# Delta rule of block 2: in-chunk products as 64x64 on the diagonal quarters of TensorE

## The chip, the core and the metric

The kernel runs on one core of a Trainium2 chip. The metric is the device time of one execution in microseconds; the time before is the median of three runs.

## The reference, cut to what matters

Two layers of block 1 and then two layers of block 2 work on x of 512 tokens by 1024. Block 2 mixes three branches (a dilated attention, a convolution, and a gated delta rule with 4 heads of 128 channels) and then has a gated feed-forward. The change is in the delta rule, which works in chunks of 64 tokens:

```python
def chunk_gated_delta_rule(q, k, v, g, beta):
    ...
    C = GDN_CHUNK                       # 64
    ...
    decay = jnp.exp(jnp.where(lower_incl, g[..., :, None] - g[..., None, :], -jnp.inf))
    k_beta = k * beta[..., None]
    v_beta = v * beta[..., None]
    m = jnp.where(strict, jnp.einsum('bhncd,bhnsd->bhncs', k_beta, k) * decay, 0.0)
    rhs = jnp.concatenate([v_beta, k_beta * jnp.exp(g)[..., None]], axis=-1)
    sol = lax.linalg.triangular_solve(m + jnp.eye(C, dtype=jnp.float32), rhs, left_side=True, lower=True,
                                      unit_diagonal=True)
    u = sol[..., :Dv]
    w = sol[..., Dv:]
    intra = jnp.where(lower_incl, jnp.einsum('bhncd,bhnsd->bhncs', q, k) * decay, 0.0)

    def step(state, xs):
        q_c, k_c, u_c, w_c, g_c, intra_c = xs
        v_new = u_c - w_c @ state
        out = (q_c * jnp.exp(g_c)[..., None]) @ state + intra_c @ v_new
        ...
```

## The kernel before

All activations lie transposed, 128 channels on the partitions by 512 tokens. A dense product is three matmuls per 128x128 weight tile, high and low parts in fp32r (`mm3`, L307 to L309); the weights come in on SP's queue and are split by ScalarE (L285) and VectorE (L286). The delta rule and the attention work in plain fp32, where one matmul leaves two records in the trace; a transpose leaves one.

Block 2's mixing (`block2_mix`) is a set of generators that a `Driver` runs while the program is built. Dense jobs (26 projections of one layer, then the output projection) yield after every three matmuls, foreground generators after every step, with the TensorE time and the latency they are assumed to have (`yield 430, 600`). The driver takes the foreground step that is due with the smallest priority number, else a dense step. So it sets TensorE's order: the steps of the delta rule stand between pieces of dense products. PSUM gives 3 tiles to dense products and 5 to everything else (`pm`).

A `Half` is two heads. Its queries, keys and values go through a short convolution on VectorE (`gdn_conv`) and through transposes (L555). `intra(b)` then works on one block of 128 tokens (two chunks) and both heads, at most two such chains at a time, four chains a half: decays from the gates (L1090), the scores k k^T and k q^T as whole 128x128 products (L1103, L1111), of which a mask leaves the two diagonal 64x64 quarters, and five levels that double the size of the inverted triangular blocks. TT is the transposed inverse; in each level it is transposed (L1118, copied to T by ScalarE, L1120), W = m T is formed (L1124, copied, L1126), then W TT (L1130), and VectorE writes it into TT under a mask (L1131). At the end w (L1136) and u (L1141) are formed. GpSimd scales the decays (L1096, L1098) and makes the first TT from m (L1107, L1108).

`rec` takes the 8 chunks of a half in order: w times the state (L1165), subtracted from u, the state's update (L1173), q times the state (L1186, scaled by VectorE, L1189), and after two chunks the score product (L1195). `out` transposes a head's result back (L1218). `ab_post` prepares the gates at the start of the layer.

## Time and profile before

| | us |
|---|---|
| median of three runs | 2601.34 (2600.72 to 2603.84) |
| profiled execution, its time | 2604.12 |
| its span | 2602.3 |
| TensorE (PE) busy | 2523.3 |
| its weight loads (PEld) | 2061.3 |
| VectorE (DVE) busy | 1535.7 |
| ScalarE (ACT) busy | 1027.9 |
| GpSimd (POOL) busy | 518.0 |

The span is what the profiler saw from the first to the last instruction. A record's duration is from its start to its modelled end; the next matmul may start well before that end, so the distance between two starts tells what a matmul takes of TensorE's time. "128\*64" in a row is rows by columns of the array in use, the shape behind it the data that stream through. The two layers' mixing stages of block 2 lie at about 1140 to 1440 us and 1880 to 2170 us.

### The profile page before, as it was taken

To read this page: it belongs to the slowest core of one execution; us is meant where nothing else is said; L and a number is where in the kernel's file an instruction comes from. 1 tells how busy PE (TensorE), PEld (TensorE's weight loads), DVE (VectorE), ACT (ScalarE), POOL (GpSimd) and SP (SyncE) were. 2 spreads that over 40 slices of the span, in tenths; PEclk is the share of its full clock that TensorE was granted. 3 is DMA by queue.
4 is the path that set the end of the run, shared out by engine and by line. 5 is a ranking of instruction groups with operands and counts; after the bars stand their busy time and mean duration, and the time that the engine had idled before them with its cause. 6 is when DMAs were issued, how large, how long until landed. Compare 5 with 4: busy or idle time off the path is not lost. (4 is left out here: it accounts for less than half of the span.)

```text
span 2602.3 us, 33506 instructions
## 1 busy us (share of the span) xinstructions
PE 2523.3 (97%) x12988; PEld 2061.3 (79%) x12988; DVE 1535.7 (59%) x2380; ACT 1027.9 (39%) x1715; POOL 518.0 (20%) x465
## 2 busy tenths in 40 slices
PE   8999999999999999999999999999899999999998
PEld 6777888878778888877777888888777778888887
DVE  6777666336776665356898554432678885744323
ACT  4554333223644333234345432222443355522221
POOL 3332111003231111013220221100221311311101
PEclk9999999999999999999999999999999999999999
DMA  4113222332022223321111222223211112222232
GB/s 165 41 42 110 96 96 96 92 103 82 33 76 95 98 97 95 116 93 40 57 41 63 84 98 97 97 91 99 96 57 41 41 49 98 82 97 97 96 95 77
DMA packets 69854, 216.05 MB, mean 83 GB/s; under 512 B 8256, under 2 KB 11968, under 8 KB 69696
## 3 DMA queue, kind: packets, MB, share of 16 engines
q1 hardware_dynamic: 68336, 212.40, 24.4%
q8 instruction: 102, 1.67, 0.3%
q10 hardware_dynamic: 1360, 1.52, 0.2%
q14 instruction: 56, 0.46, 0.1%
HBM read 207.60 MB, written 6.29 MB: 82 GB/s over the span
## 5 line engine op out<-in xcount | busy, mean ns | idle before, releaser
L307 PE MATMUL pd<-hh,wh 128*128 128x512 f32 (+1 forms) x2064 | 800.5, 391 | 12.3 <-ACT wh L285 8.1
L308 PE MATMUL pd<-hl,wh 128*128 128x512 f32 (+1 forms) x2064 | 800.6, 389 | 7.0 <-DVE hl L525 4.4
L309 PE MATMUL pd<-hh,wl 128*128 128x512 f32 (+1 forms) x2064 | 796.0, 388 | 0.9 <-DVE wl L286 0.9
L285 ACT CAST wh<-wr 128x1024 fp32r<-128x1024 f32 (+2 forms) x407 | 400.7, 986 | 976.2 <-PE pd L308 927.4
L286 DVE TENSOR_TENSOR wl<-wr,wh 128x1024 fp32r<-128x1024 f32 (+2 forms) x407 | 471.4, 1160 | 398.7 <-ACT wh L285 389.1
L308 PEld LDWEIGHTS pd<-hl,wh 128*128 128x128 f32 x2064 | 389.7, 189 | 84.1 <-DVE hl L525 7.5
L307 PEld LDWEIGHTS pd<-hh,wh 128*128 128x128 f32 x2064 | 387.3, 189 | 87.1 <-ACT wh L285 8.1
L309 PEld LDWEIGHTS pd<-hh,wl 128*128 128x128 f32 x2064 | 388.9, 189 | 75.2 <-DVE wl L286 2.0
L309 PE MATMUL pd<-gh,wl 128*128 128x512 f32 (+1 forms) x704 | 269.0, 382 | 0.0
L308 PE MATMUL pd<-gl,wh 128*128 128x512 f32 (+1 forms) x704 | 269.0, 382 | 0.0
L307 PE MATMUL pd<-gh,wh 128*128 128x512 f32 (+1 forms) x704 | 268.8, 382 | 0.0
L309 PEld LDWEIGHTS pd<-gh,wl 128*128 128x128 f32 x704 | 132.6, 188 | 28.3
L308 PEld LDWEIGHTS pd<-gl,wh 128*128 128x128 f32 x704 | 132.6, 188 | 28.3
L307 PEld LDWEIGHTS pd<-gh,wh 128*128 128x128 f32 x704 | 132.6, 188 | 28.3
L1550 POOL TENSOR_TENSOR fz<-fz,nrB 128x512 f32<-128x512 f32 x44 | 77.6, 1764 | 365.6 <-ACT fz L1549 365.6
L864 POOL TENSOR_TENSOR fy<-fy,fy 128x512 f32<-128x512 f32 x44 | 56.7, 1288 | 383.2 <-DVE fy L858 367.5
L1557 DVE TENSOR_TENSOR fz<-pd,fz 128x512 f32<-128x512 f32 x42 | 29.0, 691 | 138.4 <-PE pd L309 135.4
L854 DVE TENSOR_TENSOR fh<-pd,nrB 128x512 f32<-128x512 f32 x88 | 60.5, 687 | 59.8 <-PE pd L309 54.9
L533 POOL TENSOR_TENSOR nacc<-nacc,nsq 128x512 f32<-128x512 f32 x30 | 46.2, 1540 | 240.7 <-ACT nsq L532 240.1
L1368 DVE SCALAR_TENSOR_TENSOR cz<-cy,dwh,cz 128x501 f32<-128x501 f32 (+21 forms) x120 | 89.1, 752 | 1.2 <-ACT cz L1366 0.3
L1548 DVE TENSOR_TENSOR fz<-pd,nrB 128x512 f32<-128x512 f32 x42 | 28.8, 690 | 102.7 <-PE pd L309 102.7
L856 ACT ACTIVATE fy<-fh,cols 128x512 f32<-128x512 f32 x88 | 71.9, 817 | 35.9 <-DVE fh L854 35.9
(400 smaller groups left out, 3530.1 us busy)
## 6 DMA issues: line engine op xcount, KB each, us to landing
wr<-in_w_up_dram SPq DMA_DIRECT2D x132, 512.0 KB, 3.2
wr<-in_w_in_dram SPq DMA_DIRECT2D x80, 512.0 KB, 3.3
wr<-in_w_down_dram SPq DMA_DIRECT2D x64, 512.0 KB, 3.5
wr<-in_w_gate_dram SPq DMA_DIRECT2D x44, 512.0 KB, 3.2
wr<-in_w_down_dram SPq DMA_DIRECT2D x32, 384.0 KB, 3.1
wr<-in_w_o_dram SPq DMA_DIRECT2D x32, 256.0 KB, 2.8
wr<-in_w_out_dram SPq DMA_DIRECT2D x16, 512.0 KB, 3.3
xd<-x SPq DMA_DIRECT2D x16, 256.0 KB, 2.0
```

Source lines behind the costliest of these rows:

```text
L285: nc.scalar.copy(out=hi[:, cs], in_=raw[:, cs])
L286: nc.vector.tensor_tensor(lo[:, cs], raw[:, cs], hi[:, cs].bitcast(F32), ALU.subtract)
L307: nc.tensor.matmul(ps, wh, xhi, start=start, stop=False)
L308: nc.tensor.matmul(ps, wh, xlo, start=False, stop=False)
L309: nc.tensor.matmul(ps, wl, xhi, start=False, stop=stop)
L533: (nc.vector if last else nc.gpsimd).tensor_tensor(self.acc, self.acc, sq, ALU.add)
L854: nc.vector.tensor_tensor(h, ps, F.rB, ALU.mult)
L856: nc.scalar.activation(out=y, in_=h, func=AF.Identity, scale=col("cw1", tt), bias=col("cb", tt))
L864: nc.gpsimd.tensor_tensor(y, y, part.pop(t), ALU.mult)
L1368: nc.vector.scalar_tensor_tensor(zt[:, s:], y[:, :S - s], w(30 - s), zt[:, s:], ALU.mult, ALU.add)
L1550: nc.gpsimd.tensor_tensor(z, z, F.rB, ALU.mult)
L1557: nc.vector.tensor_tensor(z, ps, z, ALU.mult)
```

## The change

- `intra` works on two blocks (four chunks) and both heads in one chain, so a half has two chains instead of four. Of every product only the diagonal quarters are formed: eight 64x64 matmuls for two blocks, two chunks and two heads, with row r of the array's halves in turn. A tile of 256 columns holds the four blocks of one product.
- T and TT stand side by side in one tile (`both`). T comes once from TT by a product with the identity; after that each level forms W TT and TT W (16 matmuls, one masked copy of 512 columns), so that T needs no transpose in the next level.
- The decays of a half are made at once for all blocks (`decays`): one 128x512 product, and VectorE, GpSimd and ScalarE instructions of 512 columns.
- A head with odd number has its two chunks of each block swapped (`swap`): its convolution's result is written in two half-width instructions. So in one step of `rec` the two heads lie on different halves of the partitions and stand on different halves of the array.
- In `rec` both heads' shares of a chunk are 128 columns wide, on 128 partitions together; the update of the state goes into two PSUM tiles, and the scaling of q times the state goes from VectorE to ScalarE. `out` takes both heads of a half.

The diff, cut to its core:

```diff
...
+        ab, sw = tl(K, "z", 3), tl(K, "z", 3)
...
+        for c in range(2):
+            nc.scalar.copy(out=swap(sw[:64, :], c), in_=swap(ab[:64, :], 1 - c))
...
-    def gdn_conv(ps, j, tag, bufs):
+    def gdn_conv(ps, j, tag, bufs, odd):
...
-        tanh_silu2(K, th, y)
+        if not odd:
+            tanh_silu2(K, th, y)
+            return th
+        for c in range(2):
+            nc.scalar.activation(out=swap(th, c), in_=swap(y, 1 - c), func=AF.Tanh, scale=0.5)
+        for c in range(2):
+            nc.vector.scalar_tensor_tensor(swap(th, c), swap(th, c), 1.0, swap(y, 1 - c), ALU.add, ALU.mult)
...
-        def intra(self, b):
+        def decays(self):
...
+            of = lambda q: sl[self.hp][:, 8 * q:8 * q + 8].rearrange("p (n o) -> p n o", o=1).to_broadcast([128, 8, 64])
+            yield lambda: st.ab and (self.hp == 0 or halves[0].begun[1])
+            steps = tl(K, "sq", 1)
+            nc.gpsimd.tensor_tensor(e64(steps), of(0), row(K.tri64), ALU.mult)
+            yield 0, 2000
+            ps = ps_m(K)
+            nc.tensor.matmul(ps, K.same, steps, start=True, stop=True)
+            dd = tl(K, "dd", 1, n=1024)
+            dn, dt_ = dd[:, :512], dd[:, 512:]
+            nc.vector.tensor_tensor(e64(dt_), e64(ps), of(1), ALU.subtract)
+            nc.gpsimd.tensor_tensor(e64(dt_), e64(dt_), row(K.mk), ALU.add)
+            nc.scalar.activation(out=dt_, in_=dt_, func=AF.Exp)
+            nc.gpsimd.tensor_tensor(e64(dt_), e64(dt_), of(2), ALU.mult)
+            nc.gpsimd.tensor_tensor(e64(dn), e64(dt_), row(K.nstrict), ALU.mult)
+            self.dd = dd.rearrange("p (a n) -> p a n", a=2)
+            yield 860, 7000
...
+        def intra(self, bp):
             hp = self.hp
...
+            at = [(bl, c, r) for bl in range(2) for c in range(2) for r in range(2)]
+            rows = lambda r: slice(64 * r, 64 * r + 64)
+            cell = lambda bl, c: slice((2 * bl + c) * 64, (2 * bl + c) * 64 + 64)
...
+            toks = lambda bl, r: slice((2 * bp + bl) * 128 + 64 * r, (2 * bp + bl) * 128 + 64 * r + 64)
...
+            yield lambda: (st.intra < 2 and self.dd is not None and self.nk == 2 and self.q[1] is not None and
+                           (bp == 0 or self.begun[0]))
             st.intra += 1
...
             knT, q = self.knT, self.q
+            both = tl(K, "TT", 2)
+            TT, T = both[:, :256], both[:, 256:]
+            nc.gpsimd.tensor_tensor(r44(TT), K.id64.rearrange("p (o j) -> p o j", o=1).to_broadcast([128, 4, 64]),
+                                    K.id64.rearrange("p (o j) -> p o j", o=1).to_broadcast([128, 4, 64]), ALU.mult)
             pk = ps_m(K)
...
+            for n, other in enumerate((knT, q)):
+                for bl, c, r in at:
+                    h = r ^ c
+                    nc.tensor.matmul(pk[rows(r), 256 * n:256 * n + 256][:, cell(bl, c)], knT[h][:, toks(bl, r)],
+                                     other[h][:, toks(bl, r)], start=True, stop=True)
+            ma = tl(K, "AT", 3)
+            nc.vector.tensor_tensor(ma.rearrange("p (a n) -> p a n", a=2), pk.rearrange("p (a n) -> p a n", a=2),
+                                    self.dd[:, :, bp * 256:bp * 256 + 256], ALU.mult)
+            mT, self.AT[bp] = ma[:, :256], ma[:, 256:]
+            nc.vector.copy_predicated(r44(TT), K.pairs, r44(mT))
+            yield 900, 2000
+            p0 = ps_m(K)
+            for bl, c, r in at:
+                nc.tensor.matmul(p0[rows(r), cell(bl, c)], TT[rows(r), cell(bl, c)],
+                                 K.ident[rows(r), rows(r)], start=True, stop=True)
+            nc.scalar.copy(out=T, in_=p0[:, :256])
+            yield 430, 600
             for lv in range(5):
-                p0 = ps_m(K)
-                for h in range(2):
-                    nc.tensor.transpose(p0[:, hs[h]], TT[:, hs[h]], K.ident)
-                T = bt("T", 2)
-                nc.scalar.copy(out=T, in_=p0[:, :256])
-                yield 218, 600
                 pw = ps_m(K)
-                for h in range(2):
-                    nc.tensor.matmul(pw[:, hs[h]], mT[:, hs[h]], T[:, hs[h]], start=True, stop=True)
-                W = bt("W", 2)
+                for bl, c, r in at:
+                    nc.tensor.matmul(pw[rows(r), cell(bl, c)], mT[rows(r), cell(bl, c)], T[rows(r), cell(bl, c)],
+                                     start=True, stop=True)
+                W = tl(K, "W", 2, n=256)
                 nc.scalar.copy(out=W, in_=pw[:, :256])
                 yield 430, 600
                 pb = ps_m(K)
-                for h in range(2):
-                    nc.tensor.matmul(pb[:, hs[h]], W[:, hs[h]], TT[:, hs[h]], start=True, stop=True)
-                nc.vector.copy_predicated(r2(TT), K.lvl(lv), r2(pb[:, :256]))
-                yield 430, 700
+                for n, (x, y) in enumerate(((W, TT), (TT, W)) if lv < 4 else ((W, TT),)):
+                    for bl, c, r in at:
+                        nc.tensor.matmul(pb[rows(r), 256 * n:256 * n + 256][:, cell(bl, c)], x[rows(r), cell(bl, c)],
+                                         y[rows(r), cell(bl, c)], start=True, stop=True)
+                w = 512 if lv < 4 else 256
+                four = lambda t: t[:, :w].rearrange("p (a n j) -> p a n j", n=4, j=64)
+                nc.vector.copy_predicated(four(both), K.lvl(lv), four(pb))
+                yield 860 if lv < 4 else 430, 1000
             yield lambda: self.nv == 2
+            for bl, c, r in at:
+                nc.tensor.matmul(pu[rows(r), wide(bl, c)], TT[rows(r), cell(bl, c)],
+                                 self.v[r ^ c][rows(r), blk(bl)], start=True, stop=True)
+            self.U[bp] = tl(K, "u", 2)
+            nc.scalar.copy(out=self.U[bp], in_=pu)
+            pw = [ps_m(K), ps_m(K)]
+            for bl, c, r in at:
+                nc.tensor.matmul(pw[r][:, cell(bl, c)], self.kg[r ^ c][rows(r), blk(bl)],
+                                 TT[rows(r), cell(bl, c)], start=True, stop=True)
+            self.WT[bp] = tl(K, "wT", 2)
+            for r in range(2):
+                nc.scalar.copy(out=self.WT[bp][:, 256 * r:256 * r + 256], in_=pw[r][:, :256])
...
                 for c in range(2):
...
+                    rows = [slice(64 * (h ^ c), 64 * (h ^ c) + 64) for h in range(2)]
+                    order = (c, 1 - c)
+                    vf = self.U[bp][:, (2 * bl + c) * 128:(2 * bl + c) * 128 + 128]
+                    cell = slice((2 * bl + c) * 64, (2 * bl + c) * 64 + 64)
                     if s is not None:
                         pv = ps_m(K)
...
+                        for h in order:
+                            r = h ^ c
+                            nc.tensor.matmul(pv[rows[h], :128], self.WT[bp][:, 256 * r:256 * r + 256][:, cell],
                                              s[:, hs[h]], start=True, stop=True)
...
+                        nc.vector.tensor_tensor(vf, vf, pv[:, :128], ALU.subtract)
+                        yield 220, 500
                     if not (b == NB - 1 and c == 1):
...
+                        pst = [ps_m(K), ps_m(K)]
+                        for h in order:
+                            nc.tensor.matmul(pst[h][:, :128], self.kd[h][rows[h], bs], vf[rows[h], :],
                                              start=True, stop=True)
                         ns = bt("st", 2)
...
+                        for h in range(2):
+                            if s is None:
+                                nc.vector.tensor_copy(out=ns[:, hs[h]], in_=pst[h][:, :128])
+                                continue
+                            j = 16 * (h ^ c) + 4 * b + 2 * hp + h
+                            nc.vector.scalar_tensor_tensor(ns[:, hs[h]], s[:, hs[h]], egl[:, j:j + 1],
+                                                           pst[h][:, :128], ALU.mult, ALU.add)
                     if s is not None:
                         p1 = ps_m(K)
...
+                        for h in order:
+                            nc.tensor.matmul(p1[rows[h], :128], self.q[h][:, bs][:, rows[h]], s[:, hs[h]],
+                                             start=True, stop=True)
+                        nc.scalar.activation(out=o[:, hs[c]], in_=p1[:, :128], func=AF.Copy,
+                                             scale=sl[hp][:, 24 + 2 * b + c:25 + 2 * b + c])
                     s = ns
...
+                    yield 440, 300
                 p2 = ps_m(K)
...
+                for c in range(2):
+                    for r in (slice(0, 64), slice(64, 128)):
+                        cell = slice((2 * bl + c) * 64, (2 * bl + c) * 64 + 64)
+                        nc.tensor.matmul(p2[r, hs[c]], self.AT[bp][r, cell],
+                                         self.U[bp][r, (2 * bl + c) * 128:(2 * bl + c) * 128 + 128],
+                                         start=True, stop=True)
...
     for hf in halves:
-        for b in range(NB):
-            drv.spawn(hf.intra(b), 1)
+        drv.spawn(hf.decays(), 1)
+        for bp in range(2):
+            drv.spawn(hf.intra(bp), 1)
         drv.spawn(hf.rec(), 0)
...
```

The order of TensorE's instructions in the first half's chains, layer 1 of block 2, two chains in turn. Names are output, then data and weights; 128x512 rows are the dense products. Before, it reads:

```order
L1124 MATMUL pm_9658<-T_9649,mT_9591 128x128 x2
L1118 MATMUL pm_9663<-cst,TT_9606 128x128 x2
L307 MATMUL pd_9629<-hh_8808,wh_9530 128x512
L308 MATMUL pd_9629<-hl_8809,wh_9530 128x512
L1130 MATMUL pm_9671<-TT_9593,W_9661 128x128 x2
L1124 MATMUL pm_9675<-T_9666,mT_9604 128x128 x2
L309 MATMUL pd_9629<-hh_8808,wl_9531 128x512
L307 MATMUL pd_9629<-hh_8901,wh_9530 128x512
L1118 MATMUL pm_9683<-cst,TT_9593 128x128 x2
L1130 MATMUL pm_9688<-TT_9606,W_9678 128x128 x2
```

Before, transposes, W and W TT of the two chains are single pairs of 128x128 between dense pieces. After the change TensorE has in the same place:

```order
L309 MATMUL pd_9848<-hh_9087,wl_9562 128x512
L1167 MATMUL pm_9801<-TT_9579,AT_9598 64x64 x8
L1175 MATMUL pm_9812<-TT_9601,W_9784 64x64 x8
L1175 MATMUL pm_9812<-W_9784,TT_9601 64x64 x8
L1175 MATMUL pm_9830<-TT_9579,W_9810 64x64 x8
L1175 MATMUL pm_9830<-W_9810,TT_9579 64x64 x8
L1167 MATMUL pm_9852<-TT_9601,AT_9620 64x64 x8
L307 MATMUL pd_9848<-hh_9180,wh_9561 128x512
L308 MATMUL pd_9848<-hl_9181,wh_9561 128x512
L1167 MATMUL pm_9863<-TT_9579,AT_9598 64x64 x8
L309 MATMUL pd_9848<-hh_9180,wl_9562 128x512
```

Instead of L1118, L1124 and L1130 there are groups of eight 64x64 for W (L1167) and for the two products of a level (L1175, two rows each), and the transposes are gone.

The recurrence on TensorE, one chunk of the first half. Before, it reads:

```order
L1165 MATMUL pm_9999<-st_9985,wT_9876 64x128
L1118 MATMUL pm_10003<-cst,TT_9956 128x128 x2
L309 MATMUL pd_9931<-hh_8901,wl_9787 128x512
L307 MATMUL pd_9931<-hh_8994,wh_9786 128x512
L1165 MATMUL pm_9999<-st_9985,wT_9876 64x128
L308 MATMUL pd_9931<-hl_8995,wh_9786 128x512
L309 MATMUL pd_9931<-hh_8994,wl_9787 128x512
L307 MATMUL pd_9931<-hh_9087,wh_9786 128x512
L1173 MATMUL pm_10011<-u_9881,kd_9481 128x128
L1173 MATMUL pm_10011<-u_9881,kd_9545 128x128
L1186 MATMUL pm_10017<-st_9985,q_raw_9453 64x128
L1186 MATMUL pm_10017<-st_9985,q_raw_9520 64x128
```

The chunk's steps stand in that order, with dense pieces and a transpose of a chain between. After the change TensorE has for one chunk:

```order
L1219 MATMUL pm_10228<-st_10218,wT_10112 64x128 x2
L308 MATMUL pd_10177<-hl_9088,wh_10068 128x512
L309 MATMUL pd_10177<-hh_9087,wl_10069 128x512
L307 MATMUL pd_10177<-hh_9180,wh_10068 128x512
L308 MATMUL pd_10177<-hl_9181,wh_10068 128x512
L309 MATMUL pd_10177<-hh_9180,wl_10069 128x512
L1226 MATMUL pm_10236<-u_10100,kd_9576 128x128
L1226 MATMUL pm_10235<-u_10100,kd_9493 128x128
L1239 MATMUL pm_10242<-st_10218,q_raw_9549 64x128
L1239 MATMUL pm_10242<-st_10218,q_raw_9482 64x128
L1249 MATMUL pm_10249<-u_10100,AT_9598 64x128 x4
```

The chain is the same, L1165, L1173 and L1186 are now L1219, L1226 and L1239; L1226's two matmuls write two tiles, and the score product (L1249) is four 64x128 instead of two 128x128. Dense products stand between the steps in both.

ScalarE's order at the first half's first levels, layer 1. Before, it reads:

```order
L1120 COPY T_9649<-pm_9646 128x256
L1126 COPY W_9661<-pm_9658 128x256
L1120 COPY T_9666<-pm_9663 128x256
L1126 COPY W_9678<-pm_9675 128x256
L1120 COPY T_9686<-pm_9683 128x256
L889 ACTIVATE s_9626<-y_9621 128x512
L1126 COPY W_9698<-pm_9695 128x256
L1120 COPY T_9703<-pm_9700 128x256
```

Copies of T and W alternate. After the change ScalarE has:

```order
L1012 ACTIVATE sq_9630<-pm_9625 128x512
L1170 COPY W_9676<-pm_9667 128x256
L1170 COPY W_9687<-pm_9678 128x256
L1120 ACTIVATE dd_9661<-dd_9661 128x512
L1012 ACTIVATE sq_9733<-pm_9728 128x512
L1170 COPY W_9752<-pm_9743 128x256
L1170 COPY W_9784<-pm_9775 128x256
L1170 COPY W_9810<-pm_9801 128x256
```

The copies of W (L1170) follow each other, with the Exp of the second half's decays (L1120 after, tile dd) between the first level's and the second's.

## Rows read from the trace of the kernel before

**Rows 1.** Page, part 1: busy us, share of the span, instructions.

```profile
PE 2523.3 (97%) x12988; PEld 2061.3 (79%) x12988; DVE 1535.7 (59%) x2380; ACT 1027.9 (39%) x1715; POOL 518.0 (20%) x465
```

**Rows 2.** By stretch: length, busy PE, PEld, DVE, ACT, POOL, granted clock, DMA.

```profile
1140.00:1440.00 300.00, 289.20 (x1691) 231.26 (x1690) 244.07 (x479) 133.34 (x281) 61.40 (x60) 0.99 0.16 55
1880.00:2170.00 290.00, 275.20 (x1601) 219.40 (x1603) 238.72 (x470) 130.13 (x275) 60.42 (x60) 0.98 0.16 54
664.00:702.00 38.00, 37.95 (x291) 29.86 (x290) 29.67 (x53) 25.73 (x62) 8.17 (x8) 1.00 0.13 42
```

**Rows 3.** PE's timeline in the chains: start, length, line, form, count.

```profile
1183.59 0.40 PE L308 MATMUL pd<-hl,wh 128*128 128x512 f32 x1
1183.83 0.61 PE L1130 MATMUL pm<-TT,W 128*128 128x128 f32 x4
1184.27 0.61 PE L1124 MATMUL pm<-T,mT 128*128 128x128 f32 x4
...
1189.31 0.38 PE L1118 MATMUL pm<-cst,TT 128*128 128x128 f32 x2
1189.52 0.61 PE L1130 MATMUL pm<-TT,W 128*128 128x128 f32 x4
```

**Rows 4.** PE by line and form: records, busy us, mean ns, idle before.

```profile
L1165 PE MATMUL pm<-st,wT 128*64 128x128 f32 x112 | 19.9, 289 | 0.3 <-DVE st L1181 0.3
...
L1384 PE MATMUL pm<-cz,cst 128*128 128x512 f32 x8 | 3.8, 593 | 0.0
```

**Rows 5.** PE's timeline in block 1's attention, alternating column halves.

```profile
108.56 1.97 PE L684 MATMUL pm<-pT,vt 128*64 128x128 f32 x32
110.45 0.50 PE L662 MATMUL pm<-ka,qa 128*128 128x512 f32 x1
```

**Rows 6.** PE's timeline at 64 columns of data.

```profile
1144.52 0.46 PE L928 MATMUL pm<-cst,z 64*128 64x64 f32 x4
1144.90 0.50 PE L308 MATMUL pm<-hl,wh 128*128 128x512 f32 x1
```

**Rows 7.** PE's timeline where the form changes, in the recurrence.

```profile
1204.91 0.71 PE L1173 MATMUL pm<-u,kd 64*128 64x128 f32 x4
1205.55 0.71 PE L1090 MATMUL pm<-cst,gneg 128*128 128x128 f32 x4
...
1206.43 0.65 PE L1165 MATMUL pm<-st,wT 128*64 128x128 f32 x4
1207.01 0.71 PE L1090 MATMUL pm<-cst,gneg 128*128 128x128 f32 x4
...
1209.57 0.50 PE L308 MATMUL pd<-hl,wh 128*128 128x512 f32 x1
1209.91 0.40 PE L309 MATMUL pd<-hh,wl 128*128 128x512 f32 x1
```

**Rows 8.** PE's weight loads by line: idle before them, by releaser.

```profile
L1130 PEld LDWEIGHTS pm<-TT,W 128*128 128x128 f32 x320 | 42.7, 190 | 6.6 <-ACT W L1126 2.4 <-issue 0.2
L1124 PEld LDWEIGHTS pm<-T,mT 128*128 128x128 f32 x320 | 42.1, 191 | 7.3 <-ACT T L1120 4.2 <-issue 0.7
...
L1118 PEld LDWEIGHTS pm<-cst,TT 128*128 128x128 f32 x160 | 19.5, 140 | 17.0 <-POOL TT L1108 6.7 <-DVE TT L1131 5.2 <-issue 0.7
```

**Rows 9.** Other engines by line and form: count, busy us, mean ns.

```profile
L1131 DVE COPY_PREDICATED TT<-msk,pm 128x256 f32<-128x256 uint8 x80 | 35.0, 442 | 17.9 <-PE pm L1130 17.2
L1022 DVE TENSOR_TENSOR kn<-pm,kr 128x512 f32<-128x512 f32 x8 | 5.5, 690 | 5.3 <-POOL kr L461 5.3
L1189 DVE TENSOR_TENSOR o<-pm,eG 64x256 f32<-64x256 f32 x28 | 11.8, 421 | 0.5
L1029 POOL TENSOR_TENSOR kg<-kn,eG 128x512 f32<-128x512 f32 x8 | 11.6, 1446 | 6.8 <-DVE kn L1022 6.8
```

**Rows 10.** All engines' timeline at one copy of W.

```profile
1184.92 0.37 ACT L1126 COPY W<-pm 128x256 f32<-128x256 f32 x1 [0.99 <-PE pm L1124]
...
1185.34 0.52 PEld L1130 LDWEIGHTS pm<-TT,W 128*128 128x128 f32 x4
```

More of the change, by code (lines that the diff above doesn't have):

```diff
@@ L960, in g @@
             nc.vector.tensor_copy(out=G, in_=pg[:, :16])
-            nc.vector.tensor_copy(out=Gs[:, 32:64], in_=pg[:, 32:64])
+            nc.vector.tensor_copy(out=tot[:, 16:48], in_=pg[:, 32:64])
             for c in range(2):
@@ L1437, in block2_mix @@
     for hf in halves:
-        for b in range(NB):
-            drv.spawn(hf.intra(b), 1)
+        drv.spawn(hf.decays(), 1)
+        for bp in range(2):
+            drv.spawn(hf.intra(bp), 1)
         drv.spawn(hf.rec(), 0)
@@ L1443, in block2_mix @@
     for hf in halves:
-        for h in range(2):
-            drv.spawn(hf.out(h), 1)
+        drv.spawn(hf.out(), 1)
     for c in range(2):
@@ L1614, in build @@
     nc.sync.dma_start(out=cst, in_=A["cst"])
-    K.ident, K.tri, K.mk, K.nstrict, K.mk1 = (cst[:, j * 128:(j + 1) * 128] for j in range(5))
+    K.ident, K.tri, K.same = (cst[:, j * 128:(j + 1) * 128] for j in range(3))
+    K.mk, K.nstrict, K.tri64, K.id64 = (cst[:, 384 + j * 64:448 + j * 64] for j in range(4))
     K.ind = cst[:, 640:642]
```

203 lines of the change are left out of this document (86 added, 117 removed).

## The prediction

> **What bounds the kernel now.** I read the page's busy shares first. TensorE (PE) is busy 97% of the span [rows 1], so time comes off only where PE's stream of instructions gets shorter or waits less. Next comes the stretch that the change touches: the mixing stage of the two layers of block 2, some 300 and 290 us long [rows 2]. PE is busy there for 289 and 275 us, VectorE (DVE) for 244 and 239 us: DVE is second, close enough to be a rival. "Busy" counts a matmul from start to end, and ends overlap the next start, so I price PE by the distance between starts. A dense 128x512 fp32r matmul takes 0.24 us, four records of a 128x128 fp32 product 0.44 us (one fp32 matmul is two records, so 0.22 us a matmul), two transposes 0.21 us [rows 3]. What follows sums such distances over the instructions that go and come. The counts are of instructions in the program's order.
>
> **What goes from PE.** Per chain of one block: two matmuls on each of L1090, L1103, L1111, L1136, L1141 and L1195 (32 in all on each line), and five times two on L1124, L1130 and a pair of transposes on L1118. That is 6 x 32 + 2 x 160 = 512 matmuls x 0.22 = 112.6 us, and 160 transposes x 0.105 = 16.8 us. The recurrence has 56 matmuls, 112 records, on each of L1165, L1173 and L1186 (one of them in [rows 4]), 168 x 0.22 = 37.0 us: each has 64 rows or 64 columns of the array, both heads on the same ones, so they run one after the other. Together 166.4 us.
>
> **What comes.** 1088 matmuls with 64 columns of data, 960 of them 64x64 on two diagonal quarters of the array (p0, W, and both products for T and its transpose) and 128 of form 128x64 (the two scores); 360 more with 128 columns or 128-column weights (u, w, and the recurrence). They stand in pairs, one on each half. Whether halves overlap is the largest question. L684 of block 1 shows it for two column halves: 32 records on alternating halves take from 108.56 to 110.45 us, less 0.14 of changing form (below): 1.75 us, so 0.109 us for a pair of records, the price of one [rows 5]. For 64 columns of data L928 is nearest: four records hold it 0.38 us until the next start [rows 6]; less the 0.14 of changing form, four distances of 0.06 us remain. So 544 pairs x 2 x 0.06 = 65.3 us. Below this lies half of 0.109, 0.0545 us (6 us less); above it 0.078 us, with half of the 0.14 left in the four (19 us more). I take 0.06, as it was measured at this width. The others: 180 pairs x 2 x 0.109 = 39.2 us. The four products for the decays are 128x512 in plain fp32, two records of 0.59 us with 0.17 of tail [rows 4]: 4 x 2 x 0.43 = 3.4 us. Where the order splits a pair (16 slots) and for eight added small transposes, 3.2 us. Together 111.1 us, so PE's products shrink by 55.3 us.
>
> **What changing the form costs.** The rows show a price for each burst in another form. The burst of L1165 (64 columns) holds 0.58 us until the next start where four records are 0.44: 0.14 for its first weight load and for draining at its end. L1173's (128 columns of weights) holds 0.64: 0.20. So 64 columns of a first load cost 0.06 and draining 0.08. Dense runs pay as well: L308 after a burst takes 0.34 instead of 0.24 [rows 7], and 0.08 to 0.10 more for draining at the run's end; again 0.20 a run. In the program's order the form changes 308 times before and 468 times after: 63 more times into 128x128, 88 into forms with 64 columns, 9 into 64x128. So 72 x 0.20 + 88 x 0.14 = 26.7 us back, between 22 (all at 0.14) and 32 (all at 0.20). Half of the products' gain is gone; 28.6 us is left.
>
> **Waits.** A chain before is transpose, copy, product, copy, product, masked copy. The weight loads of L1118 were held 6.7 us by GpSimd's first T and 5.2 by DVE's masked copy, those of L1124 4.2 by ScalarE's copy, those of L1130 2.4 [rows 8]: 18.5 us over 240 bursts. The changed chains have 8 x 11 = 88 bursts, and the transpose, which had most of it, stays only once a chain. In proportion 6.8 us would remain, a gain of 12; the masked copy, though, is 512 wide (0.69 us for another DVE operation of that width out of PSUM, instead of 0.44 [rows 9]) and two chains follow each other more closely, so the gain may be nothing. I take 9, nearer to the proportion because the step with the most waiting goes. GpSimd's share also goes: T no longer waits for a product on it.
> Added waits: the second half's decays put an Exp into ScalarE's queue ahead of the copies of W in the second level of the first half, waiting for GpSimd, DVE and PE before it: some 0.9 + 0.2 + 0.7 + 1.4 us (the last as GpSimd's 512-wide products on L1029 [rows 9]). PE has two W bursts, two double bursts (2.9 us) and four transposes (0.4 us) meanwhile, so it is hidden; uncovered it costs a microsecond in each layer. Odd heads are written with their 64-token halves swapped, two half-width instructions for one, 0.42 + 0.42 for 0.69 on DVE [rows 9] and as much on ScalarE, twelve times, on the way to the transposes ahead of the chains: between 0 and 4 us (12 x 0.35), I take 2.
> DVE itself loses: 80 masked copies x 0.44 = 35 us become 32 x 0.69 + 16 x 0.44 = 29, and the 28 scalings on L1189 (0.42 each) go to ScalarE [rows 9], where 72 of 80 copies of T and 40 of 80 of W go (0.37 us each [rows 10]). Nothing of it is worth time as PE is the bound, but it takes nothing either.
>
> **Sum.** -55.3 + 26.7 - 9 + 2 = -35.6 us. The profiled execution took 2604.1 us, 0.1% over the median of 2601.3; from the median it gives 2566 us. With all terms at their ends (-6, -5, -3, -2 and +19, +5, +9, +2) the forecast's own range is 2550 to 2601 us.
>
> **Rivals.**
> *The quarters do not overlap.* L684's halves share their rows; a diagonal pair reads different rows, and no row of this trace shows two row halves at once (L1173 has both heads on the same rows). If such pairs run one after the other, 480 pairs x 2 x 0.06 = 57.6 us and 64 pairs x 2 x 0.109 = 14.0 us come on top: 2566 + 72 = 2638 us, slower. It decides as soon as half of the pairs fail to overlap. For it speaks that both write one PSUM tile, against it that L684's do so too. The Trainium skill, "TensorEngine Tiling (Array Packing)", Restrictions and Gotchas, says that different row tiles can't access the same PSUM bank at once; by that rule this rival is what happens, and the trace neither confirms nor excludes it. Chance 0.10, since rows and columns are both apart here.
> *The chains are laid bare.* A handoff before: PE's four records from 1184.27 on [rows 3], the last starting 0.33 later, ScalarE's copy until 1185.29, the next weights at 1185.34 [rows 10]: 0.74 us from the last start, about 1.0 through a 512-wide DVE copy. With half of that uncovered at all 88 bursts, 0.4 x 88 = 35 us, there is no gain: 2601 us. It decides at 0.4 us a burst. In places the order sets only the other chain's burst of 0.48 us between; in most it sets dense work as well. Chance 0.08.
> *The clock falls.* In bursts that use half of the array PE's clock might drop to its lower level, 1.2 GHz; the bursts' 105 us (65.3 + 39.2) would double: 2671 us. Block 1's attention at 664 to 702 us, with half-array bursts in it, was granted 1.00 [rows 2], so 0.04.
>
> **How the numbers follow.** The forecast has 0.78, of which 0.05 lies outside its ends or near no change. Differences under 0.2% (5 us) can't be told from none. Faster: 0.78 less 0.03 at its slow end, plus 0.03 that the chains cost only part, 0.78; same: 0.08; slower: the first and third rival, 0.14. The range holds the forecast and the laid-bare chains, 2550 to 2601 us, widened by the 3 us over which the runs spread, 2547 to 2604 us, and leaves out 0.14 for the two slow rivals and 0.05 of tails.
>
> **What would show it.** Right: bursts of eight 64x64 matmuls (16 records) 0.48 us from first to next start, beside 0.15 for changing form; the mixing stages 15 to 20 us shorter each, and nothing changed elsewhere. Wrong: such a burst at 0.96 us (first rival); weight loads of the chains' bursts held above 20 us in sum (second); a granted clock of 0.5 in the delta-rule stretches (third); a change of form that costs more than 0.20 us.

## The result and the profile after

The changed kernel takes 2566.96 us (median of 4 runs, 2564.82 to 2567.89) beside 2601.32 for the kernel before: a ratio of 0.9866, with a 95% interval of 0.9852 to 0.9881. The forecast was 2566. The profiled execution took 2566.2 us with a span of 2564.2, so the span shrank by 38.1 us and the median by 34.4.

"Form" below is the part of TensorE's array in use, rows by columns (128\*64); a burst is a run of products of one step; the planner is the `Driver`.

The page's first part for the changed kernel answers to [rows 1]: TensorE (PE) has 1392 more records and 40.3 us less busy time; its idle time (span less busy) went from 79.0 to 81.2 us. VectorE (DVE), the rival for the bound, stays at 59%.

```profile
PE 2483.0 (97%) x14380; PEld 2003.6 (78%) x14380; DVE 1507.5 (59%) x2320; ACT 998.0 (39%) x1627; POOL 493.1 (19%) x425
```

The stretches answer to [rows 2]. Followed by the progress of the dense work, the changed kernel is 1 us ahead when the first mixing stage begins, 16 us ahead after it and 38 us after the second: 14 and 22 us, where the prediction had 15 to 20 each. The first two lines are close to the pieces between those points, 286 us for 300 and 268 for 290; the third is block 1's attention, as before.

```profile
1138.00:1424.00 286.00, 271.98 (x2388) 203.94 (x2387) 229.04 (x450) 118.35 (x236) 47.57 (x38) 0.99 0.19 58
1864.00:2132.00 268.00, 253.71 (x2297) 190.24 (x2297) 226.38 (x438) 113.82 (x230) 46.67 (x38) 0.99 0.19 58
664.00:702.00 38.00, 37.95 (x291) 29.85 (x290) 29.64 (x53) 25.31 (x61) 8.15 (x8) 1.00 0.13 42
```

PE's timeline in the changed kernel (start, length, line, form, count) answers to [rows 3] and [rows 7]. First a burst of eight 64x64 products for T (L1160, 16 records), then a step of the recurrence: L1226 the state update, L1239 and L1219 the products with the state, L1249 the product with the scores.

```profile
1184.64 0.40 PE L308 MATMUL pd<-hl,wh 128*128 128x512 f32 x1
1184.97 0.68 PE L1160 MATMUL pm<-cst,TT 64*64 64x64 f32 x16
1185.58 0.50 PE L309 MATMUL pd<-hh,wl 128*128 128x512 f32 x1
1185.92 0.40 PE L307 MATMUL pd<-hh,wh 128*128 128x512 f32 x1
...
1243.20 0.40 PE L309 MATMUL pd<-hh,wl 128*128 128x512 f32 x1
1243.53 0.49 PE L1226 MATMUL pm<-u,kd 64*128 64x128 f32 x4
1243.95 0.44 PE L1239 MATMUL pm<-st,q_raw 128*64 128x128 f32 x4
1244.32 0.65 PE L1249 MATMUL pm<-u,AT 64*64 64x128 f32 x8
1244.90 0.49 PE L307 MATMUL pd<-hh,wh 128*128 128x512 f32 x1
```

The burst of 16 records holds PE from 1184.97 to 1185.58, 0.61 us: the 0.48 of the forecast, 0.13 for changing form. Inside it the two quarters' records start 6 to 7 ns apart, and a pair follows the pair before after 58 ns (107 behind the first pair), no more than one record alone in the run with groups of four (58 to 59 ns). The first dense product behind it takes 0.34 us to the next start. L1226, two pairs with 128 columns of data, holds 0.42; two pairs of 0.109 and a change at 0.20 are that.

### The profile page after: what moved, and what is told of

Its sections match the earlier page's. It is cut to its first block, busy times and chain, and to the rows that moved or that the text cites. A ratio compares the mean times of both kernels' runs of the same rounds, so it can differ in the third digit from the quotient of the medians.

```text
span 2564.2 us, 35965 instructions
## 1 busy us (share of the span) xinstructions
PE 2483.0 (97%) x14380; PEld 2003.6 (78%) x14380; DVE 1507.5 (59%) x2320; ACT 998.0 (39%) x1627; POOL 493.1 (19%) x425
## 5 line engine op out<-in xcount | busy, mean ns | idle before, releaser
L308 PE MATMUL pd<-hl,wh 128*128 128x512 f32 (+1 forms) x2064 | 799.6, 389 | 7.1 <-DVE hl L525 4.4
L309 PE MATMUL pd<-hh,wl 128*128 128x512 f32 (+1 forms) x2064 | 794.8, 387 | 0.9 <-DVE wl L286 0.9
L308 PEld LDWEIGHTS pd<-hl,wh 128*128 128x128 f32 x2064 | 389.2, 189 | 89.8 <-DVE hl L525 7.6
L309 PEld LDWEIGHTS pd<-hh,wl 128*128 128x128 f32 x2064 | 388.7, 189 | 78.7 <-issue 2.9
L309 PE MATMUL pd<-gh,wl 128*128 128x512 f32 (+1 forms) x704 | 268.5, 381 | 0.0
L308 PE MATMUL pd<-gl,wh 128*128 128x512 f32 (+1 forms) x704 | 268.5, 381 | 0.0
L309 PEld LDWEIGHTS pd<-gh,wl 128*128 128x128 f32 x704 | 132.3, 188 | 28.1
L308 PEld LDWEIGHTS pd<-gl,wh 128*128 128x128 f32 x704 | 132.3, 188 | 27.9
L1428 DVE SCALAR_TENSOR_TENSOR cz<-cy,dwh,cz 128x509 f32<-128x509 f32 (+21 forms) x120 | 90.7, 765 | 0.2
```

The lines of the kernel that those rows point to most:

```text
L308: nc.tensor.matmul(ps, wh, xlo, start=False, stop=False)
L309: nc.tensor.matmul(ps, wl, xhi, start=False, stop=stop)
L1428: nc.vector.scalar_tensor_tensor(zt[:, s:], y[:, :S - s], w(30 - s), zt[:, s:], ALU.mult, ALU.add)
```

## The experiments

All times are medians, to be held against 2567.0 for the changed kernel; ratios are to the kernel before in the same set of runs.

### Four and four, and two and two

```diff
-            at = [(bl, c, r) for bl in range(2) for c in range(2) for r in range(2)]
+            at = [(bl, c, r) for r in range(2) for bl in range(2) for c in range(2)]
```

> The changed kernel with the loop over the two diagonal quarters put outermost in the chains: four products on one quarter, then four on the other, instead of alternating. Same products, same steps, same 468 changes of form. Theory (the gain hangs on two quarters working at once, and PE starts matmuls in the order of the program): only the border of two groups overlaps. A burst of eight goes from 0.46 us to about 0.81 (120 bursts, 16 groups of the scores: 136 x 0.35 = 47.6 us), the 16 groups of u and w from 0.87 to 1.53 (10.5 us): +58 us on 2567, 2625 us, slower than before. Rival 1 (PE looks several matmuls ahead and finds the other quarter's work behind four of one quarter): about +19 us, 2586. Rival 2 (the gain is from fewer steps and waits, the overlap lies in PE's slack): within 5 us of 2567.

Measured: 2594.9 us, ratio 0.9974 (0.9962 to 0.9985). None of the three numbers held: +28, where the theory had +58 and the first rival, whose mechanism it is, +19. Its timeline has the same burst at 0.89 us instead of 0.61:

```profile
1185.54 0.96 PE L1160 MATMUL pm<-cst,TT 64*64 64x64 f32 x16
1186.43 0.50 PE L309 MATMUL pd<-hh,wl 128*128 128x512 f32 x1
```

In the burst the second group's first record starts 0.29 us after the first group's, 6 ns behind its fifth of eight (the next expectation says beside the sixth). The rows don't name a record's quarter; this record lasts 267 ns, as only the first on a quarter does in the bursts shown, the others 218. So PE does not wait for the turn, but it sees only some three records ahead. Summed from the first start of a stretch in one form to the first of the next, the 76 stretches of 64x64 take 108.5 us instead of 85.9, and the 39 of 64x128 take 27.4 instead of 21.8: 28.2 us, the whole difference (in the two profiles the granted clock took 3.4 us more here and PE's idle 3.6 less, see the last section). So most of the change's gain hangs on the two quarters working at once.

The look-ahead was then tested with groups of two:

```diff
-            at = [(bl, c, r) for bl in range(2) for c in range(2) for r in range(2)]
+            at = [(bl, c, r) for bl in range(2) for r in range(2) for c in range(2)]
```

> The changed kernel with the chains' products in groups of two: two on one diagonal quarter, two on the other, and so on (all in turn before, four and four in the run that took 2595 us). In that run's trace the second group's first record starts 0.29 us into the burst, beside the sixth of the first group's eight records: PE had three records of the first group still to start. Theory (PE starts another quarter's product about three records ahead of the turn): of two products, four records, only the first must have started, so a burst loses little, 0 to 0.06 us of its 0.61 in 136 bursts: 2567 to 2575 us. Rival (what is lost goes with the share of neighbours on the same quarter, half of them here, three quarters there: two thirds of the 28 us): 2586 us.

Measured: 2573.6 us, ratio 0.9887 (0.9870 to 0.9903), +6.6, inside the theory's range and 12 us from the rival. The burst is 0.65 us, 0.04 longer:

```profile
1186.00 0.73 PE L1160 MATMUL pm<-cst,TT 64*64 64x64 f32 x16
1186.65 0.50 PE L309 MATMUL pd<-hh,wl 128*128 128x512 f32 x1
```

Many bursts stand in stretches of several. Summed as above, the stretches of 64x64 take 88.7 us instead of 85.9 and those of 64x128 22.6 instead of 21.8: 3.6 us. The rest of the 6.6 need not be the order's, since the granted clock took 5.1 us more from this run's profile than from the changed kernel's.

### What a change of form costs

```diff
                 for bl, c, r in at:
+                    if (bl, c, r) == (1, 0, 0):
+                        nc.tensor.matmul(pw[:, 256:384], K.ident, K.tri, start=True, stop=True)
                     nc.tensor.matmul(pw[rows(r), cell(bl, c)], ...
```

> The changed kernel with one 128x128 fp32 product (into an unused half of the PSUM tile, its result is not used) set in the middle of each of the 40 bursts for W. It costs 0.22 us by itself, 8.8 in all. In the order of the program the form changes 547 times instead of 468: 41 more into 128x128, 36 more into 64x64, 2 into 128x64. Theory (0.20 and 0.14 us a change): 8.8 + 8.2 + 5.3 = +22.3 us, 2589. Rival 1 (changing the form is hidden, or a few ns): +9 us, 2576. Rival 2 (a change costs twice that): +36 us, 2603.

Measured: 2587.7 us, ratio 0.9944 (0.9930 to 0.9957): +20.7. Less 8.8 for the products themselves, 11.9 us for 79 changes, 0.15 each (the granted clock took 3.4 us more from this profile, and PE idled 3.0 us less). In its timeline the inserted product (L1168, two records, 0.22 in a run of its own form) holds PE for 0.42 us, and the four products behind it (the first of the 16 records of the last line, which runs into the next burst) start anew:

```profile
1188.62 0.45 PE L1169 MATMUL pm<-TT,AT 64*64 64x64 f32 x8
1189.00 0.49 PE L1168 MATMUL pm<-cst 128*128 128x128 f32 x2
1189.42 0.68 PE L1169 MATMUL pm<-TT,AT 64*64 64x64 f32 x16
```

The other way round, changes were taken out of the recurrence: p1 (q times the state) moved right behind pv (w times the state, of the same form), and p2 (the scores' product) into the step of the last state update of its block.

```diff
                         nc.vector.tensor_tensor(vf, vf, pv[:, :128], ALU.subtract)
+                        p1 = ps_m(K)
+                        for h in order:
+                            nc.tensor.matmul(p1[rows[h], :128], self.q[h][:, bs][:, rows[h]], s[:, hs[h]],
+                                             start=True, stop=True)
...
                         yield 220, 500
...
-                    if s is not None:
-                        p1 = ps_m(K)
...
                     s = ns
-                    yield 440, 300
+                    if c == 0:
+                        yield 440, 300
```

> The changed kernel with two bursts of the recurrence joined to others: p1 (form 128x64) right behind pv (the same form), and p2 (64x64) right behind the last state update of its block, without a step of the planner between. Same products. The form changes 430 times instead of 468 (29 fewer into 128x64, 8 into 128x128, 1 into 64x64). Theory (0.14 and 0.20 us a change): -5.8 us, 2561. Rival (changes of form in the recurrence lie in waits for VectorE and cost nothing there): 2567.

Measured: 2560.9 us (2560.1 to 2563.3), ratio 0.9841 (0.9826 to 0.9856): -6.1 for 38 changes, 0.16 each. In the profiles PE's busy time falls by 6.3 us, its idle rises by 0.7 and the clock takes as much from both, so it isn't a wait that went. This version beats both kernels. In its timeline p1 (L1224) follows pv (L1219) after 0.27 us, without a change, and p2 (L1249) comes right behind the update (L1232); in the changed kernel, in the result section, p1 (L1239) stood between these two with a change on either side.

```profile
1241.69 0.44 PE L1219 MATMUL pm<-st,wT 128*64 128x128 f32 x4
1241.96 0.39 PE L1224 MATMUL pm<-st,q_raw 128*64 128x128 f32 x4
1242.28 0.50 PE L308 MATMUL pd<-hl,wh 128*128 128x512 f32 x1
1242.62 0.40 PE L309 MATMUL pd<-hh,wl 128*128 128x512 f32 x1
1242.95 0.49 PE L1232 MATMUL pm<-u,kd 64*128 64x128 f32 x4
1243.37 0.65 PE L1249 MATMUL pm<-u,AT 64*64 64x128 f32 x8
```

### T and its transpose

Here T's transpose is not kept: the loop of a level is transpose (by products), copy, W, copy, one product, masked copy.

```diff
             for lv in range(5):
+                p0 = ps_m(K)
+                for bl, c, r in at:
+                    nc.tensor.matmul(p0[rows(r), cell(bl, c)], TT[rows(r), cell(bl, c)],
+                                     K.ident[rows(r), rows(r)], start=True, stop=True)
+                nc.scalar.copy(out=T, in_=p0[:, :256])
+                yield 430, 600
...
-                for n, (x, y) in enumerate(((W, TT), (TT, W)) if lv < 4 else ((W, TT),)):
...
+                for bl, c, r in at:
+                    nc.tensor.matmul(pb[rows(r), cell(bl, c)], W[rows(r), cell(bl, c)],
+                                     TT[rows(r), cell(bl, c)], start=True, stop=True)
```

> The changed kernel with T's transpose not kept: the second product of a level (32 bursts of eight) and its half of the masked copy are left out, and at each level T is made anew by eight 64x64 products with the identity and a copy on ScalarE (32 bursts of eight more). So PE has the same number of products, 32 handoffs more; in the order of the program the form changes 440 times instead of 468 (-15 into 128x128, -12 into 64x64, -1 into 128x64: -4.8 us). Theory (the step that was taken out had most of the waiting; a handoff costs 0.08 us, as 18.5 us over 240 bursts before, up to 0.17, as some 15 us over 88 bursts after): +2.5 to +5.4 of waits, less 4.8: 2565 to 2568 us, no difference. Rival (the chains lie bare, 0.4 us a handoff): +12.8 - 4.8, 2575 us.

Measured: 2569.0 us, ratio 0.9870 (0.9857 to 0.9884), +2, within 0.2%. The run has 28 fewer changes of form, worth 4.3 us at 0.155, and the granted clock took 3.4 us more from its profile; so the 32 handoffs that it adds (burst, copy, next burst) cost some 3 to 6 us, about the 2.5 to 5.4 of the theory, and the changes of form give that back. PE's rows of that run show that the wait for the masked copy goes with whatever reads T first.

```profile
L1161 PE MATMUL pm<-cst,TT 64*64 64x64 f32 x640 | 24.7, 225 | 4.7 <-DVE TT L1177 3.6 <-DVE TT L1156 1.1
L1167 PE MATMUL pm<-TT,AT 64*64 64x64 f32 x640 | 24.4, 226 | 0.6
```

### The waits of the chains

The changed kernel's rows by line (columns as in [rows 4] and [rows 8]): PE itself, its weight loads, and the masked copy. A hold is the time for which a group's weight loads stood idle for one engine.

```profile
L1167 PE MATMUL pm<-TT,AT 64*64 64x64 f32 x640 | 26.3, 223 | 3.5 <-DVE TT L1179 3.5
L1175 PE MATMUL pm<-TT,W 64*64 64x64 f32 x640 | 26.3, 221 | 1.0 <-ACT W L1170 0.9
L1179 DVE COPY_PREDICATED TT<-msk,pm 128x512 f32<-128x512 uint8 x32 | 22.6, 727 | 7.8 <-PE pm L1175 7.5
L1175 PEld LDWEIGHTS pm<-TT,W 64*64 64x64 f32 x640 | 21.9, 135 | 6.1 <-ACT W L1170 5.1
L1167 PEld LDWEIGHTS pm<-TT,AT 64*64 64x64 f32 x640 | 21.6, 134 | 13.8 <-DVE TT L1179 8.4 <-issue 2.1 <-ACT TT L1162 1.5
```

First the planner was told of a longer masked copy:

```diff
-                yield 860 if lv < 4 else 430, 1000
+                yield 860 if lv < 4 else 430, 1800
```

> The changed kernel with the planner told that the masked copy of a level takes 1.8 us instead of 1.0 until the next step of its chain, so that more dense work is set ahead of the next W burst. The form changes 478 times instead of 468 (5 more into 128x128, 5 into 128x64: +1.7 us). Theory (the 8.4 us that the W bursts' weight loads are held by DVE's masked copy are exposed because the order leaves too little work between): most of it goes, -8.4 x 0.8 + 1.7 = -5 us, 2562. Rival (VectorE's queue is late whatever stands between, or the wait moves to dense work that waits for VectorE): 2567 to 2570 us.

Measured: 2565.9 us, ratio 0.9859 (0.9846 to 0.9873), 1 us less, nearer to the rival than to the 2562 of the theory. VectorE's hold went as meant, and ScalarE's rose by almost as much. The same rows of that run:

```profile
L1175 PEld LDWEIGHTS pm<-TT,W 64*64 64x64 f32 x640 | 21.8, 134 | 13.3 <-ACT W L1170 12.9
L1167 PEld LDWEIGHTS pm<-TT,AT 64*64 64x64 f32 x640 | 21.7, 135 | 3.1 <-ACT TT L1162 1.5 <-issue 0.5 <-ACT W L1170 0.4
```

Then both steps got more time (the copy of W 1400 instead of 600):

> As the kernel in which the planner was told 1.8 us for the masked copy, and also 1.4 us instead of 0.6 for ScalarE's copy of W, so that both steps of a level have more work set behind them. The form changes 449 times instead of 468 (11 fewer into 128x128, 5 fewer into 64x64, 3 fewer into 128x64: -3.3 us). With the masked copy alone the hold moved: VectorE's fell from 8.4 to 0 us, ScalarE's for the next burst rose from 5.1 to 12.9. Theory (the wait is that of a chain too short of work behind its steps, and can be covered): both go, -11 to -13 and -3.3, 2551 to 2553 us. Rival (it moves on, to the other chain or to the dense work): 2562 to 2567.

Measured: 2565.0 us, ratio 0.9859 (0.9842 to 0.9875): 2 us, less than the 19 changes of form alone should give (2.9). The rival held: VectorE's hold was back at 7.5 us, ScalarE's fell to 3.0. Next the two chains of a pair of heads ran in one step, without dense work between:

```diff
             for lv in range(5):
...
+                W = [None, None]
+                for bp in two:
+                    pw = ps_m(K)
...
+                    nc.scalar.copy(out=W[bp], in_=pw[:, :256])
+                yield 860, 600
```

> The changed kernel with the two chains of a pair of heads run in one program of steps: at each step the burst of the first pair of blocks, then that of the second, without dense work between; one such double chain at a time instead of two single ones. Same products. In the order of the program the form changes 451 times instead of 468 (12 fewer into 128x128, 9 fewer into 64x64, 4 more into 64x128: -2.9 us). Theory (a handoff is covered when the other chain's burst is set behind it): of the 15 us that the chains' weight loads are held after the change a third to a half goes, -5 to -7.5, together 2557 to 2559 us. Rival 1 (each step now waits for two copies in a row on ScalarE or VectorE, the waits grow): 44 double steps x 0.3 us, +13 - 3, 2577 us. Rival 2 (waits and form are both in slack): 2567.

Measured: 2567.7 us, ratio 0.9866 (0.9851 to 0.9881): no difference, rival 2, though the form changes 17 times less. PE idled 5.1 us for the masked copies there (on L1175, which forms W in that run) instead of 3.5, and 0.3 for W instead of 1.0:

```profile
L1175 PE MATMUL pm<-TT,AT 64*64 64x64 f32 x640 | 25.6, 223 | 5.1 <-DVE TT L1188 5.1
```

A likely common cause, read from the traces and not tested by a run, is VectorE's queue. In the changed kernel 18 of the 40 masked copies of line 1179 start later than 0.13 us after their products' end, and in all these VectorE is at something else; summed over the 40, the delay beyond the least one (0.05 us) is 16 us. Some 3 us of it are the other chain's masked copy, as here, where two stand one behind the other, and the rest mostly convolutions and the splitting of weights:

```profile
1307.56 0.73 DVE L1428 SCALAR_TENSOR_TENSOR cz<-cy,dwh,cz 128x493 f32<-128x493 f32 x1
1308.20 1.33 DVE L1179 COPY_PREDICATED TT<-msk,pm 128x512 f32<-128x512 uint8 x2
1309.43 0.71 DVE L1428 SCALAR_TENSOR_TENSOR cz<-cy,dwh,cz 128x492 f32<-128x492 f32 x1
```

No order of PE's steps tried here shortens that queue: the same sum is 20 us with the longer masked copy told, 28 with both, and 30 with the two chains in one step.

### The swapped halves of the odd heads

```diff
-        if not odd:
+        if True:
             tanh_silu2(K, th, y)
```

> The changed kernel with the odd heads' q, k and v written like the even ones, without swapping their 64-token halves (one tanh and one VectorE product instead of two half-width ones each, twelve times less): the odd heads' data are then in the wrong order, which changes the output. The form changes 463 times instead of 468 (-0.9 us). Theory of the prediction: the swap costs 2 us (0 to 4), so 2564 (2562 to 2566). Rival (the swap delays VectorE in the convolutions, and the transposes of k wait for it: the weight loads of line 555 for kn are held 14.2 us by VectorE after the change and 7.6 before it): -6.6 - 0.9, 2559 to 2560 us.

This kernel leaves the swap out, so the odd heads' results are not the reference's and only its time says something. Measured: 2567.3 us, ratio 0.9864 (0.9850 to 0.9879), no difference from the changed kernel, so above both numbers. The rival falls: PE waits for the normalized k just as long without the swap, as the rows of the changed kernel and of this one (in that order) show.

```profile
L555 PE MATMUL pm<-cst,kn 128*128 128x128 f32 x32 | 5.2, 285 | 13.6 <-DVE kn L1046 13.6
```

```profile
L555 PE MATMUL pm<-cst,kn 128*128 128x128 f32 x32 | 5.7, 304 | 14.0 <-DVE kn L1046 14.0
```

A price of 2 to 4 us isn't excluded by this, since the granted clock took 5.1 us more from this run's profile than from the changed kernel's (last section); its four executions were granted 0.992 or 0.993, the changed kernel's 0.993 or 0.994.

### Both gains together

> Both edits that gained: p1 and p2 of the recurrence joined to other bursts (2560.9 us alone), and the planner told 1.8 us for the masked copy and 1.4 us for the copy of W (2565.0 alone, against 2567.0). The form changes 422 times instead of 468, 8 fewer than with the joined bursts alone (3 into 128x128, 4 into 64x64, 1 into 64x128: -1.3 us). Theory (the gain is by changes of form, the chains' waits stay): 2559 to 2560 us. Rival (with fewer steps of the recurrence between, the waits of the chains go too): 2550 to 2555 us.

Measured: 2566.3 us (2562.8 to 2568.2), ratio 0.9858 (0.9844 to 0.9873). A miss: the two edits don't add up, the joined bursts alone are 5 us better. Its timeline shows a place that was full before: attention's products and transposes wait for ScalarE, 1.34 and 1.01 us, and then the granted clock is down for some 7 us. The line alone is the same step in the joined kernel, without a wait.

```profile
2119.72 0.60 PE L1377 MATMUL pm<-apT,avt 128*64 128x128 f32 x4 [1.34 <-ACT apT L1371]
2120.25 0.44 PE L1369 MATMUL pm<-cst,sc 128*128 128x128 f32 x2
2121.70 0.69 PE L1369 MATMUL pm<-cst,sc 128*128 128x128 f32 x2 [1.01 <-ACT sc L1359]
```

```profile
2113.63 0.44 PE L1377 MATMUL pm<-apT,avt 128*64 128x128 f32 x4
```

```profile
2120.00:2125.00 5.00, 3.98 (x21) 2.81 (x20) 4.38 (x9) 3.14 (x10) 0.00 (x0) 0.61 0.50 157
2125.00:2130.00 5.00, 5.00 (x23) 4.09 (x23) 2.77 (x5) 2.02 (x7) 0.00 (x0) 0.71 0.00 0
```

5 x 0.39 + 5 x 0.29 = 3.4 us of clock and 2.35 of waits are 5.8 of the 7.7 us between the two profiled executions; another fall of the clock, at 1281 us, which the joined kernel lacks, takes 1.7. Of the four executions two took 2568 us at a granted clock of 0.992, the others 2564.5 and 2562.8 at 0.994 and 0.995, so part of the miss is the clock. Why the clock falls at these places wasn't tested.

## Why the prediction was right, step by step

**Products (-55.3).** Right, and shown. A pair costs 0.058 us instead of 0.06 with 64 columns of data and 0.109 with 128, so the term is -57.5 (544 x 2 x 0.002 = 2.2 better). The first rival falls: the quarters overlap although both write one PSUM tile. The rule of the Trainium skill, "TensorEngine Tiling (Array Packing)", Restrictions and Gotchas, that different row tiles can't access one PSUM bank at once, would have made it hold; the traces disagree, for tiles that write different partitions of one PSUM tile (6 to 7 ns apart). The rival's price of 72 us was an overestimate even for a kernel that doesn't alternate, since PE looks ahead: 28 us with groups of four.

**Changing the form (+26.7).** Right, and shown twice: 0.15 us by adding 79 changes, 0.16 by removing 38, where the sum had 0.17 in the mean. 160 x 0.155 = 24.8, 2 us less. The first lines of the changed kernel's timeline give a little more: L308, the burst and L309 take 0.33, 0.61 and 0.34 us from start to start; less eight pairs of 0.058 and two dense products of 0.23, some 0.35 is left for two changes.

**Waits (-9).** Here the reading was weak. The 18.5 us of [rows 8] are idle times of the weight loads, which run ahead of the products; PE's own rows in the kernel before have much less, as these show:

```profile
L1124 PE MATMUL pm<-T,mT 128*128 128x128 f32 x320 | 50.3, 284 | 0.4 <-ACT T L1120 0.4
L1118 PE MATMUL pm<-cst,TT 128*128 128x128 f32 x160 | 31.2, 281 | 6.4 <-POOL TT L1108 4.9 <-DVE TT L1131 1.3
```

With 0.1 on L1130 that is 6.9 us before and 4.5 after, and with the scores (L1103 and L1111 2.2, L1150 0.7) -3.9. What went is GpSimd's share: 4.9 us of L1118's wait were for its first T, and L1160, which makes T now, has no idle. The waits for the two copies rose, from 2.0 to 4.5.

PE's rows understate in turn: a matmul counts as busy to its end, so a wait shorter than its tail isn't seen. In the trace of before such waits can be read from the starts. In a burst on L1124 or L1130 the second record starts 0.108 us behind the first at the least, 0.214 at the most and 0.147 in the mean of 160 bursts, though no idle stands there: 0.038 x 160 = 6 us. In the changed kernel's bursts for T, W and the products of a level the second pair starts 0.059 us behind the first, 0.107 behind a change of form, and never later. With the 3.9 that makes about 10 us, taken from the traces and not from an experiment. The whole idle of the weight loads, 30.9 us in the three lines of [rows 8] against 21.7 (the two lines above and L1160's 1.8), fell by 9.2.

The proportion to the number of bursts, by which 6.8 us of named holds should have remained, failed: 15.0 remained (8.4, 1.5 and 5.1), most of it for masked copies. The argument for 9, that the step with the most waiting goes, is borne out in part: the run that makes T anew at each level pays 3 to 6 us for the step that it puts back.

**Odd heads (+2).** No difference was measured without the swap, and the clock hides whether there is one of 2 us. What did come on top stands elsewhere: PE's wait for k (13.6 instead of 10.2 us), 2.5 for the squares of the convolution's branch on L555 where there was none, 2.7 instead of 1.5 for GpSimd's row on L470; 7.1 us, other lines -1.0. The sum put these waits at nothing. Two rows of before, then two of the changed kernel:

```profile
L555 PE MATMUL pm<-cst,kn 128*128 128x128 f32 x32 | 5.5, 300 | 10.2 <-DVE kn L1022 10.2
L470 PE MATMUL pm<-cst,lnr 128*128 128x128 f32 x8 | 1.3, 285 | 1.5 <-POOL lnr L461 1.5
...
L470 PE MATMUL pm<-cst,lnr 128*128 128x128 f32 x8 | 1.3, 285 | 2.7 <-POOL lnr L461 2.7
L555 PE MATMUL pm<-cst,sq 128*128 128x128 f32 x8 | 1.3, 280 | 2.5 <-DVE sq L1452 2.5
```

Why k comes later when the swap is gone too stays open; VectorE is busy there for 4.89 of 5 us from 1160 on and 5.00 from 1170 on (3.42 between), and the stage's order differs in more than the swap.

**Exp of the second half on ScalarE, VectorE as the bound.** Hidden, as predicted: PE waits 0.9 us in all for the copies of W (above); VectorE is 80 and 84% busy in the two stages.

**Sum.** -57.5 + 24.8 = -32.7; the idle outside the chains is +6.1 (7.1 less 1.0). For the -38.1 us of the spans the chains' waits must then have fallen by 11.5, for the -34.4 of the medians by 7.8. So 9 was near, and the 10 us read from the traces bear it out to within a few us (at 0.175 for a change of form the 11.5 would be 14.7).

That the total came right to 1 us is luck in part. Two misses cancel: products and form came out 4 us better than their 28.6, the waits outside the chains 4 us worse than the 2 put down for the swap. And the two profiled executions, which lost the same to the clock (15.3 and 15.2 us, the program's end included), differ by 38.1; most executions of before on record were granted 0.995 or 0.996 of the clock and the changed kernel's 0.993 or 0.994, a difference of some 4 us that the sum didn't have. The clock also makes 3.4 of the 8 us by which the two stages differ: its falls took 1.7 us from the first before and 3.4 after, 5.1 and 3.4 from the second.

**The other rivals.** The chains weren't laid bare: PE's own idle is 4.5 us in 88 bursts, 0.05 a burst instead of 0.4. The clock in half-array bursts is not lowered: from 1185 to 1190, with bursts on quarters, it is 1.00.

## What to carry to other kernels

Work on blocks of 64 can be put on two diagonal quarters of the array at the price of one, if neighbours in PE's order alternate between the quarters: groups of two cost some 4 us of PE's time here, groups of four 28, four fifths of what this change gained. Count the changes of form in the program's order, at 0.15 us each: joining bursts of one form was worth another 6 us, where moving the chains' steps about was worth nothing. Read waits on PE's own rows and on its weight loads, as a lower and an upper bound, and look at the distances between starts for what lies between.

## What the runs showed of the hardware

**A wait can cost twice.** In the changed kernel's profile the granted clock falls to the lower level seven times, each time within 2.2 us of the end of a PE wait of 1.6 to 3.7 us; behind ten other waits of 1 us or more it does not fall. The longest is PE's wait of 3.65 us for k, in a stretch of which it is busy for 1.91 of 5 us; then:

```profile
1178.09 0.65 PE L555 MATMUL pm<-cst,kn 128*128 128x128 f32 x4 [3.65 <-DVE kn L1046]
```

```profile
1175.00:1180.00 5.00, 1.91 (x13) 1.63 (x13) 4.10 (x5) 1.19 (x3) 4.09 (x4) 0.88 0.04 17
1180.00:1185.00 5.00, 5.00 (x71) 3.73 (x69) 4.79 (x8) 0.72 (x1) 1.59 (x1) 0.78 0.34 105
1185.00:1190.00 5.00, 4.99 (x80) 3.46 (x81) 3.97 (x7) 2.49 (x6) 0.45 (x1) 1.00 0.01 3
```

5 x 0.12 + 5 x 0.22 = 1.7 us of full clock are gone there. Added up over the profiled execution of each kernel, (1 - granted clock) x time is given below, without the last fall, which stands at the program's end in all of them; PE's idle is span less busy time.

| | median us | changes of form | PE idle us | lost to the clock us |
|---|---|---|---|---|
| before | 2601.3 | 308 | 79.0 | 10.2 |
| changed | 2567.0 | 468 | 81.2 | 10.2 |
| four and four | 2594.9 | 468 | 77.6 | 13.7 |
| two and two | 2573.6 | 468 | 78.2 | 15.4 |
| a product inserted | 2587.7 | 547 | 78.2 | 13.7 |
| joined bursts | 2560.9 | 430 | 81.9 | 10.2 |
| transpose not kept | 2569.0 | 440 | 79.8 | 13.7 |
| longer masked copy told | 2565.9 | 478 | 78.2 | 10.2 |
| both told | 2565.0 | 449 | 79.6 | 13.7 |
| two chains in one step | 2567.7 | 451 | 82.3 | 11.9 |
| no swap | 2567.3 | 463 | 79.0 | 15.4 |
| both gains | 2566.3 | 422 | 86.6 | 15.4 |

Differences of 5 us between such variants can be the clock's alone, so gains of a few us were not to be read from medians without it.

**PE starts another quarter's product early.** In groups of four the second quarter's first record started 0.29 us into the burst, while three of the first quarter's eight records had yet to start.
